# Making the low parts of layer B's weights with ScalarE and an accumulating DMA

## The chip, the cores and the metric

The kernel runs on one core of one Trainium2 chip. The metric is device time in microseconds (us) of one execution, the median of several. A core has five engines that take their instructions in order from queues of their own: TensorE (PE in the profile; its weight loads are listed as PEld), VectorE (DVE), ScalarE (ACT), GpSimd (POOL) and SyncE (SP, which here only issues DMAs). They meet through semaphores, that is, one engine's instruction waits until another engine, or a DMA, has signalled.

## The reference

The reference is a trunk of two transformer-like layers on one sequence of 512 tokens, 1024 wide, in float32, with a memory of 256 tokens. Cut to what matters:

```python
for l in range(2):
    h = rmsnorm(x, norm_mix[l])
    if l == 0:                        # layer A
        proj = h @ a_w_in[0]          # gates, values, memory queries
        main = short_conv_mixer(hv, gate_b, gate_c, a_conv[0])
    else:                             # layer B
        proj = h @ b_w_q[0]           # q1, q2 and memory queries
        q1, q2 = rope(rmsnorm(q1)), rope(rmsnorm(q2))
        o = diff_attention(q1, q2, k1, k2, v, lam)   # softmax(s1) - lam * softmax(s2)
        main = rmsnorm(o, b_subln[0]) * (1 - lam_init)
    mo = memory_attention(qm, mem_n, w_mem_kv[l], ...)
    x = x + concat(main, mo) @ w_o[l]
    x = x + square(relu(rmsnorm(x, norm_mlp[l]) @ w_up[l])) @ w_down[l]
    if l == 0:
        k1, k2, v = split(rmsnorm(x, kv_norm) @ w_kv)   # k1, k2 get rmsnorm and rope too
```

## The kernel before

Every large product is done three times over. The kernel keeps each float32 operand as two float32r tiles: the high part (the value as a float32r write leaves it) and the low part (the value minus the high part). `product` (L276) then issues three matmuls for each 128x128 weight block: high weight by high data (L279), high weight by low data (L280), low weight by high data (L281). The activations stand transposed, features on the partitions and the 512 tokens along the free dimension, so one matmul streams 512 columns.

The weights are packed on the host into `wall`, in the order of use, as a list of units (`UNITS`). A unit is eight 128x128 blocks, 512 KB. There are 192 of them: layer A (`qmA`, `mkv`, `win`, `woA`), the first MLP (`up`, `dn`), layer B (`qB`: 2 units, `qk`, `kk` and `kv`: 18 units, `wo1`: 6, `wo2`: 2) and the second MLP. The 28 units of layer B are the ones that the change touches.

`prep_to` (L251) makes a unit's weights ready one half at a time (four blocks, 128x512 elements, 256 KB):

- `dma_to` (L225) loads the raw unit through SP into one of three buffers `raw`: as one DMA (L234) or, for `qB`, `qk`, `kk` and `kv`, as two (L238). For those four kinds POOL then multiplies each half by the norm's gains (L244).
- ACT copies the half into `wh` (L261), which is the high part.
- DVE subtracts `wh` from the raw half and writes `wl`, the low part (L263). For `wo1`, and for one unit of the second MLP that is called `side`, POOL does that subtraction.

`wh` and `wl` have four buffers each, and a half is prepared three halves ahead of its use (`AHEAD`). So the writes of a half wait until PE has finished with the half four places earlier, and PE takes it up three halves after that. A raw buffer is free for the next load when both halves of its unit have been read, that is, when the second `wl` is done.

In layer B the products of the weights (`gemm_pieces`, L283; `wo1`, L972; `wo2`, L995) are interleaved with attention. A small planner (`later`, `drive`, `next_task`) runs the attention's pieces as tasks that come due after so many weight blocks. The pieces that the steps of the prediction touch are:

- head norms (`HeadNorm`, L480): ACT squares (L495, L496), DVE low parts (L497), PE sums, reciprocal roots (L416 to L420), then DVE scales the heads (L525) and `split` (L345) makes high and low parts on ACT (L346) and DVE (L347);
- rotary embedding of a pair's queries and keys: row DMAs out (L940), a DVE shuffle (L951), three POOL operations (L952 to L954), row DMAs back (L946);
- memory attention (L585): DVE maxima (L620), ACT exponentials (L623), transposes (L594), products `mov` (L603);
- differential attention (L657): score products `sc` (L583), DVE maxima (L705), ACT exponentials (L708) and scaling (L712), DVE combination `pm` (L713), PE transposes `tp` (L677), their split `th`, `tl` (L346, L347), products `o` (L690), ACT eviction (L693);
- the norm of the attention's output (`subln`, L631): ACT squares (L638, L639), DVE low part (L640), PE sums `oss` (L645, L646), root (L416 to L420), DVE scaling `ob` (L648) and split into `hh`, `hl`, which the products of `wo1` or `wo2` wait for.

What the source emits is put into each engine's queue by a scheduler when the program is built; in the trace the order on an engine is close to the order of the source, though not the same.

Of the kernel before, what the change touches and what calls it, by code (L numbers as in the profile page):

```python
# [10 lines left out]
F32 = mybir.dt.float32  # L11
F32R = mybir.dt.float32r
AF = mybir.ActivationFunctionType
ALU = mybir.AluOpType
# [21 lines left out]
WO_B = (2, 3)  # L36
SEG = 4
AHEAD = 3
LO_ON_POOL = ("wo1",)
WARM = 9  # L40

SUMS, ROOTS, NEXT_ROOT, VT = 5, 8, 3, 2
# [21 lines left out]
def _unit_list():  # L64

    u = []
    u += [("qmA", t, KT) for t in range(2)]
    for m in range(NH):
        if m == MEMA:
            u += [("mkv", 0, t, KT) for t in range(4)]  # L70
        if m == MEMB:
            u += [("mkv", 1, t, KT) for t in range(4)]
        u += [("win", CONV + m * P, KT), ("win", 2 * CONV + m * P, KT), ("win", m * P, KT)]
    u += [("woA", d, KT) for d in range(KT)]

    def mlp(l):
        r = []
        for q in range(NF):
            r += [("up", l, q * KT + f, KT) for f in range(KT)]
            r += [("dn", l, q, d, KT) for d in range(KT)]  # L80
        return r

    u += mlp(0)
    u += [("qB", 768 + t * P, KT) for t in range(2)]
    for p, t in LAYER_B:
        if t < 4:
            u += [("qk" if t < 2 else "kk", p * P + (t % 2) * 64, KT)]
        else:
            u += [("kv", 768 + (2 * p + t - 4) * P, KT)]
    u += [("wo1", i, KT) for i in range(len(WO1) // KT)]  # L90
    u += [("wo2", i, KT) for i in range(len(WO2) // KT)]
    u += mlp(1)
    return u


UNITS = _unit_list()
# [95 lines left out]
def trunk_kernel(ctx: ExitStack, tc: tile.TileContext, xT, memT, wall, cst, shp, csn, out):  # L192
    nc = tc.nc
    act, dve, pool, pe = nc.scalar, nc.vector, nc.gpsimd, nc.tensor
# [24 lines left out]
    side = next(i for i, u in enumerate(UNITS) if u[:2] == ("up", 1))  # L219
# [5 lines left out]
    def dma_to(n, between=()):  # L225
        between = list(between)
        while st["dma"] <= min(n, len(UNITS) - 1):
            i = st["dma"]
            kind, nb = UNITS[i][0], UNITS[i][-1]
            r = wpool.tile([P, KT, P], F32, tag="raw", name="raw", bufs=3)  # L230
            src = wall[OFFS[i] : OFFS[i] + P * P * nb].rearrange("(p b n) -> p b n", p=P, n=P)
            step = SEG if i < 2 or kind in ("qB", "kv", "qk", "kk") else nb
            if step == nb:
                nc.sync.dma_start(out=r[:, :nb, :], in_=src)  # L234
            for b0 in range(0, nb, step):
                rs = r[:, b0 : min(nb, b0 + step), :]
                if step < nb:
                    nc.sync.dma_start(out=rs, in_=src[:, b0 : min(nb, b0 + step), :])  # L238
                    for f in between[:2]:
                        f()  # L240
                    between = between[2:]
                if kind in ("qB", "kv", "qk", "kk"):
                    g0 = C_MIX1 if kind in ("qB", "qk") else C_KV
                    pool.tensor_tensor(  # L244
                        out=rs, in0=rs,
                        in1=cs[:, g0 + b0 : g0 + b0 + step].unsqueeze(2).to_broadcast([P, step, P]),
                        op=ALU.mult)
            st["raw"][i] = r
            st["dma"] += 1

    def prep_to(n):  # L251
        while st["prep"] <= min(n, len(halves) - 1):
            i, h = halves[st["prep"]]
            dma_to(i + 1)
            r = st["raw"][i]
            b0, b1 = h * SEG, min(UNITS[i][-1], h * SEG + SEG)
            rs = r[:, b0:b1, :]
            wh = wpool.tile([P, SEG, P], F32R, tag="wh", name="wh", bufs=4)
            wl = wpool.tile([P, SEG, P], F32R, tag="wl", name="wl", bufs=4)
            n_ = b1 - b0  # L260
            act.activation(out=wh[:, :n_, :], in_=rs, func=AF.Copy)  # L261
            eng = pool if i == side or UNITS[i][0] in LO_ON_POOL else dve
            eng.tensor_tensor(out=wl[:, :n_, :], in0=rs, in1=wh[:, :n_, :].bitcast(F32), op=ALU.subtract)  # L263
            st["w"][(i, h)] = (wh, wl)
            st["prep"] += 1

# [2 lines left out]
    def weights(b):  # L269

        i, b = cur["u"] + b // KT, b % KT
        prep_to(first[(i, b // SEG)] + AHEAD)
        wh, wl = st["w"][(i, b // SEG)]
        return wh[:, b % SEG, :], wl[:, b % SEG, :]
# [8 lines left out]
    def gemm_pieces(ps, srcs, order=range(KT), step=1, cols=slice(None)):  # L283

        u = cur["u"]
        cur["u"] += cols.stop in (None, S)
        for j, b in enumerate(order):
            prep_to(first[(u, b // SEG)] + AHEAD)
            wh, wl = (w_[:, b % SEG, :] for w_ in st["w"][(u, b // SEG)])
            product(ps, (wh, wl), [x_[:, cols] for x_ in srcs[b]], j == 0, j == len(order) - 1)  # L290
            if j % step == step - 1:
                yield
# [765 lines left out]
```

## Time and profile before

| | |
|---|---|
| median of 3 runs | 1149.05 us (1148.96 to 1150.08) |
| the profiled execution, its own time | 1151.81 us |
| its span, first to last instruction | 1150.0 us, 14438 instructions |
| PE busy over the span | 1134.6 us |
| DVE, ACT, POOL busy over the span | 660.2, 534.8, 125.4 us |
| mean granted TensorE clock | 0.995 of full speed |

The profile is one execution, recorded by the hardware. A row of the timeline gives start, duration, engine, line, operation, output and inputs; in square brackets stands how long the engine had been idle just before, and what ended that wait. A row of the groups gives how many instructions of one kind there are, their busy time together, the mean of one in ns, the idle time before them and what ended it. A row of the windows gives the busy time of PE, PEld, DVE, ACT and POOL in one stretch, then the granted TensorE clock (PEclk), the DMA engines' share and GB/s. The strips on the page cut the span into 40 equal slices of 28.75 us; each digit is the busy share in tenths. Matmuls overlap in the records: each lasts 0.39 us, while one starts every 0.23 us. So a busy PE may still lose time to small gaps, and a wait that matters shows as a bracket on a PE row.

### The profile page before, as it was taken

How to read it: one execution, taken by the hardware profiler on the slowest of the kernel's cores; microseconds unless marked ns; L12 is line 12 of the kernel's file. 1: busy time of each engine (PE TensorE's matmuls, PEld its weight loads, DVE VectorE, ACT ScalarE, POOL GpSimd, SP SyncE). 2: the span in 40 equal slices, each digit the busy share in tenths (PEclk: the TensorE clock that was granted, in tenths of full speed). 3: DMA queues.
4: the chain of work that ended last, by engine and by line, in shares of the span. 5: the costliest groups of instructions: out<-in, count | busy, mean ns of one | idle time of the engine just before them, and what ended most of it. 6: DMA issues, size and time to landing. Idle time of an engine off the chain costs nothing.

```text
span 1150.0 us, 14438 instructions
## 1 busy us (share of the span) xinstructions
PE 1134.6 (99%) x5343; PEld 929.2 (81%) x5343; DVE 660.2 (57%) x1106; ACT 534.8 (47%) x1037; POOL 125.4 (11%) x130
## 2 busy tenths in 40 slices
PE   8999999999999999999999999999999999999998
PEld 6888888888888888888887777678788888888887
DVE  7876664643453443445778899877643543443442
ACT  6656544542342342344577777666532432432431
POOL 3100002000000000003433332224000000000000
PEclk9999999999999999999999999999999999999999
DMA  7232333223322322324322123212232233223231
GB/s 267 99 111 73 103 109 101 92 92 103 99 92 95 107 92 92 106 97 137 119 83 67 62 70 106 92 56 74 94 108 92 92 101 102 92 94 106 94 112 71
DMA packets 38983, 113.64 MB, mean 99 GB/s; under 512 B 4992, under 2 KB 6528, under 8 KB 38912
## 3 DMA queue, kind: packets, MB, share of 16 engines
q1 hardware_dynamic: 38912, 112.71, 29.7%
q8 instruction: 42, 0.69, 0.2%
q14 instruction: 29, 0.24, 0.1%
HBM read 106.93 MB, written 4.19 MB: 97 GB/s over the span
## 4 chain that ended last, share of the span: by engine, by line
PE 84%; DVE 5%; ACT 2%; issue 1%; ACTq 0%; DVEq 0%
PE g L279 26%; PE g L280 26%; PE g L281 26%; PE sc L583 1%; PE mov L603 1%; PE o L690 1%; DVE wl L263 1%; DVE xl L436 1%; PE mtp L594 1%; PE msc L583 0%; DVE ra L420 0%; PE tp L677 0%; DVE dnb L705 0%; ACT pm L708 0%; DVE x L1018 0%
## 5 line engine op out<-in xcount | busy, mean ns | idle before, releaser
L261 ACT ACTIVATE wh<-raw 128x512 fp32r<-128x512 f32 x384 | 241.9, 631 | 487.5 <-PE g L280 428.8
L263 DVE TENSOR_TENSOR wl<-raw,wh 128x512 fp32r<-128x512 f32 x370 | 263.3, 712 | 175.6 <-ACT wh L261 174.6
L279 PE MATMUL g<-xh,wh 128*128 128x512 f32 x816 | 323.0, 396 | 0.4 <-DVE x L1018 0.4
L280 PE MATMUL g<-xl,wh 128*128 128x512 f32 x816 | 320.0, 392 | 3.1 <-DVE xl L436 3.0
L281 PE MATMUL g<-xh,wl 128*128 128x512 f32 x816 | 319.1, 391 | 0.0
L279 PE MATMUL g<-hh,wh 128*128 128x512 f32 (+1 forms) x632 | 246.3, 390 | 1.8 <-ACT hh L346 1.8
L280 PE MATMUL g<-hl,wh 128*128 128x512 f32 (+1 forms) x632 | 245.4, 388 | 0.0
L281 PE MATMUL g<-hh,wl 128*128 128x512 f32 (+1 forms) x632 | 245.1, 388 | 0.0
L280 PEld LDWEIGHTS g<-xl,wh 128*128 128x128 f32 x816 | 153.6, 188 | 36.8 <-DVE xl L436 6.1
L279 PEld LDWEIGHTS g<-xh,wh 128*128 128x128 f32 x816 | 153.8, 188 | 35.9 <-issue 2.5
L281 PEld LDWEIGHTS g<-xh,wl 128*128 128x128 f32 x816 | 153.6, 188 | 32.3 <-DVE wl L263 0.3
L279 PEld LDWEIGHTS g<-hh,wh 128*128 128x128 f32 x632 | 119.1, 188 | 27.4 <-ACT hh L346 2.1
L280 PEld LDWEIGHTS g<-hl,wh 128*128 128x128 f32 x632 | 119.3, 189 | 24.3 <-DVE dsm L711 0.6
L281 PEld LDWEIGHTS g<-hh,wl 128*128 128x128 f32 x632 | 119.3, 189 | 24.0
L772 DVE TENSOR_TENSOR x<-x,g 128x512 f32<-128x512 f32 (+1 forms) x65 | 44.1, 679 | 105.4 <-PE g L281 105.4
L762 DVE SCALAR_TENSOR_TENSOR v<-g,rstd 128x512 f32<-128x512 f32 x64 | 44.1, 691 | 90.7 <-PE g L281 90.7
L765 DVE TENSOR_TENSOR hl<-a,hh 128x512 fp32r<-128x512 f32 x64 | 44.4, 694 | 38.0 <-ACT a L764 38.0
L455 POOL TENSOR_TENSOR acc<-acc,sqf 128x512 f32<-128x512 f32 x18 | 24.7, 1372 | 368.6 <-ACT sqf L443 368.2
L244 POOL TENSOR_TENSOR raw<-raw,cs 128x512 f32<-128x512 f32 x40 | 45.7, 1161 | 79.8 <-DMA raw<-in_wall_dram 49.1
L763 ACT ACTIVATE hh<-v 128x512 fp32r<-128x512 f32 x64 | 40.4, 632 | 19.5 <-DVE v L762 19.5
L764 ACT ACTIVATE a<-v 128x512 f32<-128x512 f32 x64 | 39.3, 615 | 0.0
L708 ACT ACTIVATE pm<-sc,dnb 128x128 f32<-128x128 f32 (+3 forms) x48 | 24.8, 519 | 7.7 <-DVE dnb L705 7.6
(277 smaller groups left out, 1014.6 us busy)
## 6 DMA issues: line engine op xcount, KB each, us to landing
raw<-in_wall_dram SPq DMA_DIRECT2D x170, 512.0 KB, 3.5
raw<-in_wall_dram SPq DMA_DIRECT2D x44, 256.0 KB, 3.0
x<-x SPq DMA_DIRECT2D x16, 256.0 KB, 2.6
x<-in_xT_dram SPq DMA_DIRECT2D x8, 256.0 KB, 5.2
out_dram<-x SPq DMA_DIRECT2D x7, 256.0 KB, 2.1
mraw<-in_memT_dram SPq DMA_DIRECT2D x4, 256.0 KB, 5.8
rc<-qp SPq DMA_DIRECT2D x24, 32.0 KB, 1.9
qp<-rc SPq DMA_DIRECT2D x24, 32.0 KB, 2.0
```

Of the source, the lines that this page charges most:

```text
L244: pool.tensor_tensor(out=rs, in0=rs, in1=cs[:, g0 + b0 : g0 + b0 + step].unsqueeze(2).to_broadcast([P, step, P]), op=ALU.mult)
L261: act.activation(out=wh[:, :n_, :], in_=rs, func=AF.Copy)
L263: eng.tensor_tensor(out=wl[:, :n_, :], in0=rs, in1=wh[:, :n_, :].bitcast(F32), op=ALU.subtract)
L279: pe.matmul(out=ps, lhsT=wh, rhs=xh, start=start, stop=False)
L280: pe.matmul(out=ps, lhsT=wh, rhs=xl, start=False, stop=False)
L281: pe.matmul(out=ps, lhsT=wl, rhs=xh, start=False, stop=stop)
L708: act.activation(out=pm[:, m, 0:n], in_=sc[m][:, 0:n], func=AF.Exp, bias=nb[:, m : m + 1], accum_out=sm[:, m : m + 1])
L762: dve.scalar_tensor_tensor(out=v, in0=ps, scalar=0.0, in1=rstd, op0=ALU.max, op1=ALU.mult)
L763: act.activation(out=hh, in_=v, func=AF.Square)
L764: act.activation(out=a, in_=v, func=AF.Square)
L765: dve.tensor_tensor(out=hl, in0=a, in1=hh.bitcast(F32), op=ALU.subtract)
L772: dve.tensor_tensor(out=x[d][:, c], in0=x[d][:, c], in1=ps[:, c], op=ALU.add)
```

## The change

```diff
-LO_ON_POOL = ("wo1",)
+LO_BY_DMA = ("qB", "qk", "kk", "kv", "wo1", "wo2")
...
             wh = wpool.tile([P, SEG, P], F32R, tag="wh", name="wh", bufs=4)
             wl = wpool.tile([P, SEG, P], F32R, tag="wl", name="wl", bufs=4)
             n_ = b1 - b0
-            act.activation(out=wh[:, :n_, :], in_=rs, func=AF.Copy)
-            eng = pool if i == side or UNITS[i][0] in LO_ON_POOL else dve
-            eng.tensor_tensor(out=wl[:, :n_, :], in0=rs, in1=wh[:, :n_, :].bitcast(F32), op=ALU.subtract)
+            if UNITS[i][0] in LO_BY_DMA:
+
+                act.activation(out=wl[:, :n_, :], in_=rs, func=AF.Copy, scale=-1.0)
+                pool.dma_start(out=wl[:, :n_, :].bitcast(F32), in_=rs, accum_op=ALU.add)
+                act.activation(out=wh[:, :n_, :], in_=rs, func=AF.Copy)
+            else:
+                act.activation(out=wh[:, :n_, :], in_=rs, func=AF.Copy)
+                eng = pool if i == side else dve
+                eng.tensor_tensor(out=wl[:, :n_, :], in0=rs, in1=wh[:, :n_, :].bitcast(F32), op=ALU.subtract)
```

For the 56 halves of layer B's 28 units, ACT first writes minus the raw half into `wl` as float32r, which is minus the high part. A DMA that POOL issues then adds the raw half to it in place, so that `wl` holds raw minus high. ACT's copy into `wh` follows. The subtraction on DVE (44 of these halves) or POOL (the 12 halves of `wo1`) is gone. All other units keep their old way, and so does `side`.

## The prediction

> **What bounds the kernel now.** I read the page first, then busy times by stage, then PE's waits in layer B.
>
> ```profile
> span 1150.0 us, 14438 instructions
> PE 1134.6 (99%) x5343; PEld 929.2 (81%) x5343; DVE 660.2 (57%) x1106; ACT 534.8 (47%) x1037; POOL 125.4 (11%) x130
> ...
> DVE  7876664643453443445778899877643543443442
> ACT  6656544542342342344577777666532432432431
> ```
>
> PE is busy 1134.6 of 1150.0 us. An edit that leaves PE's work alone can only win what PE loses by waiting and by a slower clock. DVE is full in the slices around 630 to 720 us, which is layer B; there I asked for the stage.
>
> ```profile
> 540.00:575.00 35.00, 35.00 (x155) 28.59 (x154) 25.27 (x31) 18.17 (x32) 17.68 (x16) 1.00 0.36 121
> 575.00:775.00 200.00, 193.98 (x1022) 150.26 (x1021) 170.22 (x364) 144.65 (x351) 63.29 (x69) 0.98 0.24 77
> 775.00:815.00 40.00, 38.27 (x191) 30.71 (x191) 31.08 (x46) 23.60 (x45) 11.73 (x8) 1.00 0.24 79
> ```
>
> From 575 to 775 us, where attention runs between the products, PE misses 6.0 of 200 us and DVE is busy 85%, ACT 72%. Whom PE waits for (window 540 to 830 us):
>
> ```profile
> PE g L279 <- ACT hh L346: 1.8, 1, 1.8
> PE tp L677 <- DVE tl L347: 1.2, 1, 1.2
> PE tp L677 <- DVE pm L713: 1.2, 2, 0.6
> ...
> PE mov L603 <- ACT mp L623: 0.7, 1, 0.7
> ```
>
> Those four rows make 4.9 us, all at the end of chains that go back and forth between DVE and ACT. The weights themselves are never waited for here. So the change acts by making these chains shorter or longer, and by bringing weights late or not.
>
> **What it removes.** In the groups of 575 to 775 us:
>
> ```profile
> L261 ACT ACTIVATE wh<-raw 128x512 fp32r<-128x512 f32 x43 | 27.0, 628 | 20.3 <-PE g L280 15.5 <-issue 4.5
> L263 DVE TENSOR_TENSOR wl<-raw,wh 128x512 fp32r<-128x512 f32 x32 | 25.8, 807 | 2.6 <-ACT wh L261 2.4
> ...
> L263 POOL TENSOR_TENSOR wl<-raw,wh 128x512 fp32r<-128x512 f32 x12 | 16.0, 1336 | 42.4 <-ACT wh L261 33.8 <-PE tp L677 8.5
> ```
>
> DVE loses 32 x 0.807 = 25.8 us, and falls from 170.2 to 144.4 us of 200. POOL loses 16.0 us of subtractions. Those also slow DVE, which shows at the longest wait:
>
> ```profile
> 738.90 1.29 POOL L263 TENSOR_TENSOR wl<-raw,wh 128x512 fp32r<-128x512 f32 x1 [3.12 <-ACT wh L261]
> 740.71 1.26 POOL L263 TENSOR_TENSOR wl<-raw,wh 128x512 fp32r<-128x512 f32 x1 [0.52 <-ACT wh L261]
> ...
> 739.29 1.45 DVE L420 SCALAR_TENSOR_TENSOR ra<-ra,ry 128x512 f32<-128x512 f32 x1
> 740.77 1.75 DVE L648 SCALAR_TENSOR_TENSOR ob<-ob,sub_g,ra 128x512 f32<-128x512 f32 x1
> ...
> 743.24 0.59 PE L279 MATMUL g<-hh,wh 128*128 128x512 f32 x1 [1.75 <-ACT hh L346]
> ...
> L420 DVE SCALAR_TENSOR_TENSOR ra<-ra,ry x13: 417/674/1653, 71.2 to 784.3; 8x512 f32<-8x512 f32 x6, 128x512 f32<-128x512 f32 x5, 128x256 f32<-128x256 f32 x2
> L648 DVE SCALAR_TENSOR_TENSOR ob<-ob,sub_g,ra x7: 475/737/1749, 673.4 to 785.2; 128x512 f32<-128x512 f32 x5, 128x256 f32<-128x256 f32 x2
> ```
>
> The two DVE steps that PE waits for at 743.24 take 1.45 and 1.75 us, each beside a POOL subtraction; their medians are 0.674 and 0.737. Without the subtractions the chain is 0.78 + 1.01 = 1.79 us shorter, about the whole wait of 1.75. [...]
>
> The wait at 743.24 costs more than itself, since the clock falls behind it:
>
> ```profile
> 743.00:748.00 5.00, 4.76 (x11) 2.50 (x12) 3.76 (x11) 2.25 (x7) 0.00 (x0) 0.55 0.02 7
> 748.00:752.00 4.00, 4.00 (x19) 3.32 (x18) 1.93 (x5) 2.58 (x7) 1.53 (x3) 0.71 0.00 0
> ...
> 660.00:700.00 40.00, 37.81 (x189) 29.00 (x187) 38.55 (x77) 29.80 (x66) 13.11 (x15) 1.00 0.24 73
> ```
>
> That is 5 x 0.45 + 4 x 0.29 = 3.4 us of lost matmul time. The other waits, of which the longest is 1.23 (below), lie in stretches with a clock of 1.00; so I take 1.2 us as harmless and 1.75 as enough. [...]
>
> The three other waits have a low part's subtraction on DVE ahead of them:
>
> ```profile
> 616.76 1.40 DVE L263 TENSOR_TENSOR wl<-raw,wh 128x512 fp32r<-128x512 f32 x1
> ...
> 620.93 0.39 PE L603 MATMUL mov<-mth,mh 128*128 128x256 f32 x1 [0.65 <-ACT mp L623]
> ...
> 666.27 0.67 DVE L263 TENSOR_TENSOR wl<-raw,wh 128x512 fp32r<-128x512 f32 x1
> ...
> 668.96 0.66 PE L677 MATMUL tp<-sh,pm 128*128 128x128 f32 x4 [1.23 <-DVE tl L347]
> ...
> 690.09 0.66 DVE L263 TENSOR_TENSOR wl<-raw,wh 128x512 fp32r<-128x512 f32 x1
> ...
> 692.69 0.41 PE L677 MATMUL tp<-sh,pm 128*128 128x128 f32 x2 [0.63 <-DVE pm L713]
> ```
>
> At 620.93 the removed 1.40 covers the wait of 0.65: -0.65. At 668.96, with a wait of 1.23, the removed 0.67 shifts L713 and `tl`, but L713 also waits for ACT, so I take -0.5. At 692.69 the removed 0.66 covers 0.63: -0.6. What is late next at these places is ACT's part of the same chains.
>
> **What it adds on ACT.** One more activation per half: 43 x 0.628 = 27.0 us from 575 to 775. ACT goes from 144.7 to 171.7 of 200 us, 86%, just what DVE has now. Chains that DVE held up will now be held up by ACT, queued behind one activation more. Beside these, ACT stands still in front of a `wh` until PE frees it, and `wl` is freed one matmul later (0.23 us), so what is queued there (softmax, splits) starts up to 0.9 us later. From below this costs nothing, where ACT's idle 55 us absorb it; from above it brings back what DVE's load cost, 0.65 + 1.2 + 1.2 = 3.1 us of waits. ACT's load comes out so near to DVE's that I take a value towards the upper end, 2.5 us.
>
> **What it adds on POOL and the DMAs.** 56 DMAs of 256 KB. The trace has no DMA issued by POOL and none that adds. Issue: I take 1.3 us, POOL's subtraction (1.29), since the issue takes its place in the queue. Transfer: the nearest rows are
>
> ```profile
> raw<-in_wall_dram SPq DMA_DIRECT2D x44, 256.0 KB, 3.0
> x<-x SPq DMA_DIRECT2D x16, 256.0 KB, 2.6
> ```
>
> 2.6 us for the same size is the lower end; an adding DMA also reads what it adds to, so 2 x 2.6 = 5.2 is the upper. I take 3.0, nearer to the lower, since both rows are mostly not data: 512 KB takes little more than 256. Together 4.3 us from ACT's end, between 3.9 and 6.5. The cover is what PE still has ahead of it. The tightest place is the first half of `qB`:
>
> ```profile
> 547.36 0.39 PE L281 MATMUL g<-hh,wl 128*128 128x512 f32 x1
> ...
> 547.56 0.63 ACT L261 ACTIVATE wh<-raw 128x512 fp32r<-128x512 f32 x1 [0.62 <-PE g L280]
> ...
> 556.20 0.39 PE L281 MATMUL g<-xh,wl 128*128 128x512 f32 x1
> ```
>
> Its `wl` buffer is free at 547.75, and PE reads the new one at 556.20: 8.45 us. Less 0.25 for the start and 0.63 on ACT, 7.6 us are left for issue and transfer, and 4.3 fits, with 3.3 over for the queue on POOL. Queued behind an issue that waits for ACT are the gain multiplications (two, 2.04 us), the rotary steps and memsets; their own waits are for earlier PE work. While attention runs, PE takes longer over three halves and the cover grows. A raw buffer comes free 3.6 us later (4.3 less 0.69 on DVE). Cover:
>
> ```profile
> 547.17 0.80 SPq L238 DMA_DIRECT2D raw<-in_wall_dram  x2
> ...
> 550.01 2.04 POOL L244 TENSOR_TENSOR raw<-raw,cs 128x512 f32<-128x512 f32 x2 [1.70 <-DMA raw<-in_wall_dram]
> ...
> 558.44 0.63 ACT L261 ACTIVATE wh<-raw 128x512 fp32r<-128x512 f32 x1 [0.62 <-PE g L280]
> ```
>
> This load's gains are in at 552.05 and ACT reads it at 558.44: 6.4 us spare. So I cost the DMAs at nothing; without cover each microsecond of lateness is paid once per round of four buffers.
>
> **The sum.** -1.75 (wait at 743) - 3.4 (clock) - 0.65 - 0.5 - 0.6 = -6.9; ACT +2.5; together -4.4, with rounding -4.5. The span goes from 1150.0 to 1145.5, the profiled run from 1151.81 to 1147.3. The runs' median is 1149.05, 2.76 below the profiled run; I take the difference over: **1144.5 us**. A measurement of this kernel tells a change from none at about 0.2%, 2.3 us. The case's own range is 1140.5 (ACT's cost at nothing, -6.9, and 1.6 us more where small gaps close too) to 1146.7 (ACT's cost at 3.1 gives 1145.3; from 1146.7 on it would count as no change).
>
> **The rivals.** (1) ACT takes DVE's place altogether. For it: 86% of ACT against DVE's 85%. Against: POOL stretches DVE's rows, and ACT's stay at 0.628. The short waits stay (0), a wait of ACT as long as 1.75 keeps the clock's drop: about 1149. (2) The chain at 743 shortens, but a gap elsewhere, or the end of layer B, brings the drop: -4.5 + 3.4 = -1.1, so 1148. For it: one gap over some 1.2 us is enough, and the order of the queues may shift.
>
> (3) Slower: the weights come late. The place is where PE runs products alone, 540 to 575 and 775 to 815 us, some 12 halves, three rounds of four buffers. It decides from 7.6 us between ACT's end and the landing. At 9.6, 2 us over, PE loses 3 x 2 = 6.0, and as gaps of 2 us are over 1.75 the clock drops once, 3.4: with the forecast's -4.5 this is +4.9, **1154 us**. For it: no row shows an adding DMA, and POOL's queue has 2.04 us of multiplications and 1.29 us additions in the same stretch. Against: the upper end, 6.5, is under 7.6. An issue that had to wait out one DVE instruction, 1.75 us at most above, would come to 4.3 + 1.75 = 6.1, still under 7.6; three in a row make 9.6. [...]
>
> **How the numbers follow.** Forecast 0.52; rivals (1) and (2) 0.12 each, both within 0.2%; (3) 0.24, which is slower. Range 1140.5 to 1154.5: the forecast whole but for a tail, the same cases, and (3) up to 9.6 us; beyond that I leave about 0.13, below 0.05.
>
> **What would show it.** Right: the wait for `hh` at 743 gone or under 1.2, and PEclk 1.00 around it; DVE near 144 and ACT near 172 us in that stretch; landing within 6.5 us of ACT's end; no PE wait for a `wl`. Wrong: PE's L281 waiting for a DMA between 540 and 575, or ACT behind more than 3.1 us of PE's waits.

## The result and the profile after

| | before | after |
|---|---|---|
| median (range) | 1149.57 us (1148.96 to 1150.34, 4 runs) | 1162.13 us (1160.24 to 1164.07, 4 runs) |
| profiled execution, span | 1151.81, 1150.0 us | 1162.33, 1160.2 us |
| PE busy, mean granted clock | 1134.6 us, 0.995 | 1135.0 us, 0.993 |

The ratio is 1.0115, with a 95% interval of 1.0100 to 1.0131: the change makes the kernel about 13 us slower. The forecast was 1144.5 us in a range up to 1154.5. It was wrong, in sign as well.

What stood from L261 on stands six lines lower now. New are L263, ACT's write of minus the high part; L264, the adding DMA, and L265, ACT's `wh` beside it. The three matmuls are L285 to L287; the gains (L244) and the loads (L234, L238) keep their lines. From the page of the changed kernel come the engines' busy time, POOL's DMA queue, the group of the new DMAs and their issue row (KB each, median us from issue to landing):

```profile
PE 1135.0 (98%) x5343; PEld 931.2 (80%) x5343; DVE 630.3 (54%) x1062; ACT 560.4 (48%) x1093; POOL 154.3 (13%) x174
...
q0 software_dynamic: 8064, 14.68, 7.5%
...
L264 POOL DMA_DIRECT2D wl<-raw x56 | 51.6, 942 | 64.7 <-ACT wl L263 38.7
...
wl<-raw POOLq DMA_DIRECT2D x56, 256.0 KB, 3.5
```

PE's work is the same. The span is 10.2 us longer, of which PE's busy time makes 0.4 and its idle time 9.8 (1160.2 - 1135.0 = 25.2, where it was 1150.0 - 1134.6 = 15.4). The DMAs themselves cost no more than the prediction gave them: 0.94 us on POOL, and 3.5 from the start of the issue to the landing, where it had 4.3 for both. The same stages as before (PE, PEld, DVE, ACT, POOL busy, then PEclk):

```profile
540.00:575.00 35.00, 33.39 (x146) 26.99 (x145) 18.97 (x20) 20.52 (x36) 20.69 (x19) 1.00 0.60 149
575.00:775.00 200.00, 185.89 (x980) 145.67 (x979) 140.06 (x314) 156.79 (x377) 83.81 (x104) 0.97 0.58 133
775.00:815.00 40.00, 39.38 (x206) 31.78 (x205) 28.91 (x49) 30.31 (x62) 16.65 (x14) 1.00 0.47 117
```

From 540 to 775 us PE is busy 33.39 + 185.89 = 219.3 us, where it was 229.0. Neither DVE nor ACT is full there. The longest of PE's waits, as the view of waits sums them (us in total, times, longest):

```profile
PE g L287 <- DMA wl<-raw: 5.1, 2, 3.5
PE tp L683 <- DVE pm L719: 4.4, 1, 4.4
PE hss L516 <- DVE sl L503: 3.4, 1, 3.4
```

They make 12.9 us. The wait for `hh` at 743 is no longer among them. Behind two of these waits, the longest of each of the first two rows, the granted clock (after POOL's figures) is lower:

```profile
575.00:590.00 15.00, 11.47 (x39) 8.95 (x38) 7.06 (x9) 7.59 (x15) 8.02 (x8) 0.77 0.42 102
721.00:728.00 7.00, 6.29 (x32) 5.35 (x33) 5.29 (x15) 6.00 (x16) 3.59 (x6) 0.76 0.47 83
```

Counted as in the prediction, that is 15 x 0.23 + 7 x 0.24 = 5.1 us more. In the kernel before, the waits read there and the clock made 4.9 + 3.4 = 8.3 us. The difference, 18.0 - 8.3 = 9.7, is about the 10.2 us of the span. So two new things have to be explained: weights that come late, and steps of DVE that do.

**Late weights.** The chain of waits of the changed kernel, in order of time, runs without PE from 552 to 582 us (start, duration, what; cut to the long pieces):

```profile
552.24 3.62 DMA wl<-raw
...
556.01 3.39 DMA raw<-in_wall_dram
...
559.57 0.51 POOL raw L244
560.08 0.96 issue
561.04 3.27 DMA wl<-raw
...
564.45 3.28 DMA raw<-in_wall_dram
...
567.90 0.53 POOL raw L244
568.43 0.94 issue
569.37 3.27 DMA wl<-raw
...
572.78 4.65 DMA raw<-in_wall_dram
...
577.60 0.53 POOL raw L244
```

It goes round: an adding DMA lands and frees a raw buffer, the load into that buffer runs, POOL multiplies the gains into it, and only then is the next adding DMA issued. Each round takes 8.3 to 9.7 us (from 561.04 to 569.37, and on to 579.11), and one unit passes per round. PE uses up a unit in 24 matmuls, 5.5 us. Why the DMA waits for a load of other data, POOL's timeline shows, with a row of ACT and one of PE:

```profile
567.90 1.51 POOL L244 TENSOR_TENSOR raw<-raw,cs 128x512 f32<-128x512 f32 x1 [4.09 <-DMA raw<-in_wall_dram]
569.37 0.87 POOL L264 DMA_DIRECT2D wl<-raw  x1
569.97 1.33 POOL L244 TENSOR_TENSOR raw<-raw,cs 128x512 f32<-128x512 f32 x1
570.96 1.18 POOL L264 DMA_DIRECT2D wl<-raw  x1
577.60 1.56 POOL L244 TENSOR_TENSOR raw<-raw,cs 128x512 f32<-128x512 f32 x1 [5.46 <-DMA raw<-in_wall_dram]
579.11 0.86 POOL L264 DMA_DIRECT2D wl<-raw  x1
...
567.53 0.61 ACT L263 ACTIVATE wl<-raw 128x512 fp32r<-128x512 f32 x1
...
582.42 0.80 PE L287 MATMUL g<-xh,wl 128*128 128x512 f32 x1 [3.53 <-DMA wl<-raw]
```

POOL's queue alternates gain, DMA, gain, DMA. The DMA issued at 579.11 is the eighth; ACT had written its `wl` at 568.14. It stood 11 us behind the gain of a unit two places later, and that gain stood 5.46 us for its load. PE's wait of 3.53 us ends with this DMA. In the source the eighth DMA comes ahead of that gain; the scheduler put the gain first.

**Late steps of DVE.** SP's waits in the changed kernel, and rows of DVE's and SP's timelines:

```profile
SPq L238 <- DMA wl<-raw: 91.3, 18, 9.5
SPq L234 <- DMA wl<-raw: 65.3, 11, 10.4
```

```profile
612.34 0.01 DVE L957 LOAD_MASK_SELECT rp<-rc  x1 [7.77 <-DMA rc<-qp]
612.36 0.72 DVE L957 STREAM_SHUFFLE rp<-rc 128x512 f32<-128x512 f32 x1
612.99 0.67 DVE L503 TENSOR_TENSOR sl<-sf,sh__5140 128x512 fp32r<-128x512 f32 x1
```

```profile
608.05 0.83 SPq L238 DMA_DIRECT2D raw<-in_wall_dram  x2
608.99 1.15 SPq L946 DMA_DIRECT2D rc<-qp  x2
...
711.25 1.66 SPq L946 DMA_DIRECT2D rc<-qp  x2
```

A load that waits for its raw buffer holds up everything behind it on SP, the row DMAs of the rotary part (L946) among them. DVE had written the rows at 604.44; their DMAs were issued behind the load, at 608.99, and DVE stands 7.77 us in front of the shuffle that needs them. At 717.9 it stands 4.93 us again, but there the queue is the smaller part. The rows were written at 709.01, their DMAs issued 2.2 us later, and these landed only 6.4 and 6.0 us after their issue, where no other takes over 3.4 (all lie between 1.8 and 2.0 in the kernel before). The DMA engines are 0.88 busy from 714 to 718 us. Queued behind on DVE are `sl`, for which PE waits 3.35 us at 613.71, and `pm`, for which it waits 4.36 us at 721.71.

### The profile page after: what moved, and what is told of

Its sections match the earlier page's. It is cut to its first block, busy times and chain, and to the rows that moved or that the text cites. A ratio compares the mean times of both kernels' runs of the same rounds, so it can differ in the third digit from the quotient of the medians.

```text
span 1160.2 us, 14562 instructions
## 1 busy us (share of the span) xinstructions
PE 1135.0 (98%) x5343; PEld 931.2 (80%) x5343; DVE 630.3 (54%) x1062; ACT 560.4 (48%) x1093; POOL 154.3 (13%) x174
## 4 chain that ended last, share of the span: by engine, by line
PE 80%; DMA 4%; ACT 3%; DVE 2%; issue 1%; POOL 1%; SPq 0%; POOLq 0%; DVEq 0%; ACTq 0%
PE g L285 25%; PE g L286 25%; PE g L287 25%; DMA raw<-in_wall_dram 2%; DMA wl<-raw 2%; PE o L696 1%; PE sc L589 1%; POOL raw L244 1%; DMA rc<-qp 1%; PE mov L609 1%; DVE xl L442 1%; PE msc L589 0%; ACT pm L714 0%; PE tp L683 0%; ACT mp L633 0%
## 5 line engine op out<-in xcount | busy, mean ns | idle before, releaser
L287 PE MATMUL g<-xh,wl 128*128 128x512 f32 x816 | 320.3, 393 | 5.1 <-DMA wl<-raw 5.1
L285 PE MATMUL g<-xh,wh 128*128 128x512 f32 x816 | 324.2, 398 | 0.5 <-DVE x L1024 0.4
L269 DVE TENSOR_TENSOR wl<-raw,wh 128x512 fp32r<-128x512 f32 x326 | 227.6, 699 | 170.4 <-ACT wh L267 169.4
L285 PE MATMUL g<-hh,wh 128*128 128x512 f32 (+1 forms) x632 | 245.6, 389 | 0.0
L287 PE MATMUL g<-hh,wl 128*128 128x512 f32 (+1 forms) x632 | 244.4, 387 | 0.0
L287 PEld LDWEIGHTS g<-xh,wl 128*128 128x128 f32 x816 | 154.4, 189 | 38.5 <-DMA wl<-raw 6.0
L285 PEld LDWEIGHTS g<-xh,wh 128*128 128x128 f32 x816 | 154.6, 189 | 36.1 <-issue 2.5
L285 PEld LDWEIGHTS g<-hh,wh 128*128 128x128 f32 x632 | 118.7, 188 | 25.2 <-issue 1.2
L287 PEld LDWEIGHTS g<-hh,wl 128*128 128x128 f32 x632 | 118.7, 188 | 24.2 <-issue 0.4
L264 POOL DMA_DIRECT2D wl<-raw x56 | 51.6, 942 | 64.7 <-ACT wl L263 38.7
L244 POOL TENSOR_TENSOR raw<-raw,cs 128x512 f32<-128x512 f32 x40 | 46.1, 1171 | 71.8 <-DMA raw<-in_wall_dram 70.6
L265 ACT ACTIVATE wh<-raw 128x512 fp32r<-128x512 f32 x56 | 35.1, 628 | 17.3 <-PE g L286 16.5
```

The source lines that it names most:

```text
L244: pool.tensor_tensor(out=rs, in0=rs, in1=cs[:, g0 + b0 : g0 + b0 + step].unsqueeze(2).to_broadcast([P, step, P]), op=ALU.mult)
L264: pool.dma_start(out=wl[:, :n_, :].bitcast(F32), in_=rs, accum_op=ALU.add)
L285: pe.matmul(out=ps, lhsT=wh, rhs=xh, start=start, stop=False)
L287: pe.matmul(out=ps, lhsT=wl, rhs=xh, start=False, stop=stop)
```

## The experiments

Theory T1: the order of in-order queues. Something that waits (a gain, a load) stands ahead of what it indirectly waits for, or of what others need. Rivals: T2, ACT's 56 added activations; T3, the adding DMAs' own price, by issue or traffic. T4 came up on the way: POOL's gains behind an issue hold DVE's operations up. Unless a diff says otherwise the base is the changed kernel; ratios are to the kernel before on the same chip, with 95% intervals.

### ACT's load without the DMAs

```diff
-                pool.dma_start(out=wl[:, :n_, :].bitcast(F32), in_=rs, accum_op=ALU.add)
                 act.activation(out=wh[:, :n_, :], in_=rs, func=AF.Copy)
+                eng = pool if UNITS[i][0] == "wo1" else dve
+                eng.tensor_tensor(out=wl[:, :n_, :], in0=rs, in1=wl[:, :n_, :].bitcast(F32), op=ALU.add)
```

> ACT writes minus the high part as in the changed kernel, but DVE (GpSimd for wo1) adds the weight to it in place, and no DMA does: ACT's load of the change without its DMAs. T1: 1148-1153, near the kernel before. T2: near the changed kernel, 1159-1165. T3: near the kernel before, 1148-1153.

Measured: 1149.29 us, 0.9999 (0.9990 to 1.0008). ACT is busy 167.55 us of 575 to 775, more than in the changed kernel, and nothing is lost. T2 falls.

### One half of the change at a time

```diff
-LO_BY_DMA = ("qB", "qk", "kk", "kv", "wo1", "wo2")
+LO_BY_DMA = ("wo1", "wo2")
```

> Only the 16 halves of wo1 and wo2 (no gains on POOL) are made by ACT and an adding DMA; the 40 halves of qB, qk, kk and kv are subtracted by DVE, as before. T1: the loop needs gains and adding DMA on the same units, so it is not there, and the row DMAs stand behind loads no longer than before: 1144-1150, below or at the kernel before, as the wait at 743 goes. T2: 16 of 56 added activations, but in the stretch where ACT is fullest: 1150-1155. T3: 16 of 56 of the loss of 12.6, or 1151-1155.

Measured: 1146.54 us, 0.9972 (0.9963 to 0.9982): faster than the kernel before, by 3.2 us. Its stage with attention:

```profile
575.00:775.00 200.00, 197.14 (x1051) 153.97 (x1050) 166.84 (x368) 154.52 (x373) 59.57 (x71) 1.00 0.35 95
```

PE is busy 197.14 us, 3.2 more than before, at a clock of 1.00 in place of 0.98, and the wait for `hh` is gone. Most of this win is the clock's: over all runs its mean goes from 0.9968 to 0.9991, which is some 2.7 us of the span (an estimate from these two means). The other half:

```diff
-LO_BY_DMA = ("qB", "qk", "kk", "kv", "wo1", "wo2")
+LO_BY_DMA = ("qB", "qk", "kk", "kv")
...
-                eng = pool if i == side else dve
+                eng = pool if i == side or UNITS[i][0] == "wo1" else dve
```

> Only the 40 halves of qB, qk, kk and kv, which have gains on POOL, are made by ACT and an adding DMA; wo1 is subtracted on GpSimd and wo2 on DVE, as before. T1 and T4: these 40 hold the whole loss and give up what wo1 and wo2 alone gained (3.0 us): 1160-1166. T3 (a price for each adding DMA): 40 of 56 of the loss of 12.6, 1157-1160.

Measured: 1166.85 us, 1.0143 (1.0121 to 1.0165). PE waits 5.8 us for weights in four places and 1.8 us for `hh`. The whole loss is in the kinds that have gains on POOL, and the 16 other DMAs win; an equal price for each DMA (T3) does not fit.

### The source's order on POOL

```diff
-                    pool.tensor_tensor(
-                        out=rs, in0=rs,
+                    with tc.issue_after(st["add"]) if "add" in st else ExitStack():
+                        pool.tensor_tensor(
+                            out=rs, in0=rs,
...
-                pool.dma_start(out=wl[:, :n_, :].bitcast(F32), in_=rs, accum_op=ALU.add)
+                st["add"] = pool.dma_start(out=wl[:, :n_, :].bitcast(F32), in_=rs, accum_op=ALU.add).ins
```

> The changed kernel with one thing more: each unit's gain multiplications are queued on POOL behind the adding DMAs of the unit before, as the source writes them. T1 (POOL's queue has a unit's gains ahead of the DMA that must free the raw buffer for the next load, so that one unit of weights passes per round of some 8.4 us, where PE uses one up in 5.5): two units pass per round, the waits of 1.8 and 3.7 us at 570 to 582 go with the clock drop behind them, SP's queue stands less, and the time falls from 1162 to 1145-1153. T2 (ACT's 56 added activations make it late): no change, 1160-1164. T3 (the adding DMAs are too slow or take too much of the DMA engines): no change, 1160-1164.

Measured: 1162.62 us, 1.0123 (1.0104 to 1.0142). T1's number was missed by 10 us, yet its first half came true: no PE product waits for weights, POOL stands 12.1 us in front of gains for loads where it stood 70.6, and PE is busy 34.63 of the 35 us from 540 to 575. The longest sums of PE's waits are now for DVE's `pm` (2.8 us) and `tl` (1.9). DVE still stands once, 4.1 us, for row DMAs, and more often its own operations last long. A stretch of DVE's and of POOL's timeline in this run, 603 to 613 us:

```profile
606.27 0.67 DVE L627 TENSOR_REDUCE nb<-msc 128x2 f32<-128x512 f32 x1
606.87 3.01 DVE L427 SCALAR_TENSOR_TENSOR ra<-ra,ry 8x512 f32<-8x512 f32 x1
```

```profile
606.39 0.87 POOL L265 DMA_DIRECT2D wl<-raw  x1 [0.40 <-ACT wl L264]
607.00 2.33 POOL L245 TENSOR_TENSOR raw<-raw,cs 128x512 f32<-128x512 f32 x2
```

An operation of 0.67 us lasts 3.01, until POOL's two gains are done. Between 540 and 815 us ten operations of DVE last 2.0 to 4.5 us here; in the kernel before none lasts over 1.8, in the changed kernel three do. T4 is that DVE gets no turn where gains follow an issue directly; how much of the 13 us these operations make was not measured.

### The row DMAs away from SP

```diff
-            nc.sync.dma_start(out=c["rc"][t * 32 + m * 16 : t * 32 + m * 16 + 16, :], in_=qn[r, :])
+            act.dma_start(out=c["rc"][t * 32 + m * 16 : t * 32 + m * 16 + 16, :], in_=qn[r, :])
```

> The changed kernel, with the row DMAs of the rotary part issued from ACT's queue in place of SP's, so that they stand behind no weight load. T1: the loop of gains, adding DMA and load stays (the first waits at 570 to 582 as in the changed kernel, 5.4 us and 3.4 of clock), but DVE's stands of 7.8 and 4.9 us in front of the shuffle go, and with them PE's waits at 613 and 721 (7.8 us and 1.7 of clock): 1151-1156. T2 and T3: 1160-1164, since neither has anything to do with SP's queue.

The edit moves the rows on their way out; the DMAs that bring them back (L952) stay on SP. Measured: 1159.58 us, 1.0092 (1.0077 to 1.0107), a smaller gain than expected. The mechanism was there: DVE no longer stands in front of the shuffle, and the waits for `sl` and `pm` fall from 3.4 and 4.4 to 0.2 and 0.6 us. But PE now waits 9.1 us for weights, in five places, where it was 5.1 in two. The loop had been hidden behind the other waits. And DVE stands 8.3 us, in two places, for the rows on their way back, for which it never stood in the changed kernel. The longer stand, 5.96 us, is POOL's queue again: the shuffle was done at 666.24, but the first rotary step stood behind a gain and started at 674.29.

### Four raw buffers

```diff
-            r = wpool.tile([P, KT, P], F32, tag="raw", name="raw", bufs=3)
+            r = wpool.tile([P, KT, P], F32, tag="raw", name="raw", bufs=4)
```

and a few small tiles shared to make room.

> The changed kernel with four raw buffers in place of three (room made by sharing one scratch tile of the root, the memory's root factor and two small softmax tiles with others). T1: a load needs the landing of a DMA two units back, so the waits of PE for weights at 570 to 582 go, and SP's queue stands less: 1147-1154 if that is all. T4: the DVE operations of 2 to 3.5 us stay, so 1153-1161. T3: 1160-1164.

Measured: 1156.66 us, 1.0058 (1.0042 to 1.0075). About half of the loss goes. Two waits for weights remain (3.4 us), and DVE still stands 8.2 us for `rc` once. POOL stands in front of gains for loads nearly as long as before the edit, 68.8 us where it was 70.6: the scheduler placed the gains earlier for it. In the changed kernel POOL has mostly done the gains of three or four later halves when it issues a half's DMA; here it is five or six.

### Gain and DMA by turns

The gains of the next unit are queued one by one ahead of this unit's two DMAs: gain, DMA, gain, DMA, so that the gains of two later halves are ahead of each DMA, in place of three or four.

```diff
...
+                gains(1)
-                pool.dma_start(out=wl[:, :n_, :].bitcast(F32), in_=rs, accum_op=ALU.add)
+                queued(lambda: pool.dma_start(out=wl[:, :n_, :].bitcast(F32), in_=rs, accum_op=ALU.add))
```

> The changed kernel with POOL's queue in the order gain, adding DMA, gain, adding DMA: the loop of one unit per round is gone as with the source's order, but two gains never follow one issue. T4: DVE's long operations shrink from some 3.2 us to about 2, so part of the loss goes: 1152-1158. T1 alone: 1145-1153. T3: 1160-1164.

Measured: 1155.76 us, 1.0045 (1.0027 to 1.0063). No PE product waits for weights, as in the run before with the source's order. Of DVE's operations six last over 2 us in place of ten, five of them 2.1 to 2.6, one 5.4. DVE still stands once, 4.3 us, for row DMAs. The loss shrinks as the held operations get fewer, which agrees with T4; what else the new order changes was not separated.

### Gains on DVE

```diff
-                    pool.tensor_tensor(
+                    dve.tensor_tensor(
                         out=rs, in0=rs,
```

> The changed kernel with the 40 gain multiplications on DVE in place of POOL, which then has the adding DMAs and little else in layer B's weights. Since the run with the source's order on POOL lost as much as the changed kernel though no PE product waited for weights any more, a new theory T4 stands beside T1: a POOL multiplication directly behind the issue of an adding DMA keeps DVE's two-operand operations from finishing until POOL pauses (3.0 to 4.5 us for an operation of 0.68), and what queues behind them on DVE reaches PE late. T4: without POOL multiplications no DVE operation lasts over 2 us, the adding DMAs no longer stand behind gains, and the time is 1144-1152, though DVE carries 27 us more. T1 alone (only the order of POOL's queue): 1145-1152 too, but then the run with the source's order should have been there. T3 (the adding DMA itself, by its issue or its traffic): 1157-1164.

Measured: 1165.68 us, 1.0141 (1.0116 to 1.0165). The held operations are gone but for one over 2 us, and no product waits for weights; but the time is no better (the profiled run is the longest of the six, 1172.25). DVE's timeline (561 to 574 us) and a row of PE's:

```profile
567.45 1.29 DVE L244 TENSOR_TENSOR raw<-raw,cs 128x512 f32<-128x512 f32 x2 [5.35 <-DMA raw<-in_wall_dram]
568.66 0.74 DVE L414 SCALAR_TENSOR_TENSOR ra<-ss,eps_c,ry 128x512 f32<-128x512 f32 x1
```

```profile
572.37 0.79 PE L515 MATMUL hss<-sh__4788,indr 128*128 128x512 f32 x1 [4.25 <-ACT sh__4788 L501]
```

The same queue fault, on another engine: DVE stands 5.35 us in front of a gain for its load, the norm's root is queued behind, and PE waits 4.25 us at the end of that chain. Over the run DVE stands 35.0 us in 18 places for such loads.

### Both at once

> The changed kernel with four raw buffers and the gains on DVE, both at once. With the gains on DVE alone, DVE stood up to 5.4 us in front of a gain for its load, whose buffer an adding DMA had not yet freed: the same loop on another engine. T1 with T4 (the loop, and DVE's operations held by POOL): the fourth buffer gives each load a round more, so DVE stands little in front of gains, no operation lasts over 2.6 us, and the time is 1144-1151. T3 (the adding DMAs' own price): 1155-1164. If one of the two theories is wrong the time stays near that of four buffers alone, 1156.

The edits are those of the run with four raw buffers and of the run with the gains on DVE. Measured: 1166.75 us, 1.0148 (1.0129 to 1.0167). A miss: DVE stands 34.3 us in 17 places, as much as with three buffers. A buffer more is no cure here: with it the scheduler placed the gains earlier on DVE too.

### An issue between the gains of the kernel before

In the kernel before:

```diff
...
+                    with tc.issue_after(g) if b0 else ExitStack():
+                        if b0:
+                            g = pool.dma_start(out=scr, in_=eps_c).ins
+                    with tc.issue_after(g) if b0 else ExitStack():
+                        g = pool.tensor_tensor(
...
```

> The kernel before, with all its subtractions, and one more thing: between the two gain multiplications of a unit GpSimd issues a DMA of 8 bytes a partition into a scratch tile that nothing reads (20 of them). No buffer waits for it and it moves nothing. T4: DVE operations that start beside such an issue last 2.0 to 2.6 us, as in the alternating run, and the time rises by 1-6 us: 1150.5-1156. T1 alone, and T3 by traffic: no DVE operation over 1.9 us, and 1148.5-1150.5.

Measured: 1151.99 us, 1.0027 (1.0012 to 1.0041), at the foot of T4's range. The issue of 8 bytes a partition takes 0.58 us. Four operations of DVE last 2.1 to 2.9 us, three of them at 539 to 553 us, where PE loses little (34.78 of 35 us busy). In the kernel before none is that long. So held operations are there without any weight depending on a DMA. The edit as a whole, 20 issues and the order that it forces, costs 3.1 us by the ratio (1.4 to 4.7). The 56 of the changed kernel are longer; whether T4 alone makes the whole loss with the source's order, this run can't say.

### Late gains

```diff
-                    pool.tensor_tensor(
-                        out=rs, in0=rs,
-                        in1=cs[:, g0 + b0 : g0 + b0 + step].unsqueeze(2).to_broadcast([P, step, P]),
-                        op=ALU.mult)
+                    st["gains"][(i, b0 // SEG)] = cs[:, g0 + b0 : g0 + b0 + step].unsqueeze(2).to_broadcast([P, step, P])
...
+            if (i, h) in st["gains"]:
+                last = [x for x in nc.cur_bb.bb.instructions if x.engine == mybir.EngineType.DVE][-1]
+                with tc.issue_after(last):
+                    dve.tensor_tensor(out=rs, in0=rs, in1=st["gains"][(i, h)], op=ALU.mult)
             if UNITS[i][0] in LO_BY_DMA:
```

> The changed kernel (three raw buffers) with the gains on DVE, and each gain queued only when its half is converted, one unit later than where the load is asked for. With gains on DVE placed as early as the buffers allow, DVE stood 34 us in all in front of gains for their loads, with three raw buffers and with four. T1 in its wider form (an in-order queue holds an instruction ahead of what it indirectly waits for, whatever the engine and the number of buffers): the load has been under way for a unit when the gain's turn comes, DVE stands less than 10 us there, and the time is 1145-1153. T3 (the adding DMAs' own price): 1157-1166, since the queue would then not be the cause.

Measured: 1149.68 us, 0.9996 (0.9986 to 1.0006). The loss of 13 us is gone, with all 56 adding DMAs in place, landing in a median of 3.7 us, and with the 40 gains (a median of 0.68 us) on DVE, which is busy 643.1 us where it was 630.3. DVE stands nowhere in front of a gain for a load. The run with the gains on DVE above differs from this one only in where the gains stand in DVE's queue, and took 1165.68 us: there the place alone makes some 16 us. The stages:

```profile
540.00:575.00 35.00, 34.61 (x150) 27.68 (x150) 19.76 (x29) 18.98 (x35) 11.30 (x11) 1.00 0.61 148
575.00:775.00 200.00, 196.18 (x1034) 151.63 (x1033) 161.78 (x365) 168.95 (x403) 55.46 (x76) 1.00 0.61 139
```

T3 falls as the cause of the loss: the DMA engines are as busy as in the changed kernel (0.61), and PE works 196.18 of 200 us. For PE's weights 0.4 us of waiting is left in the whole run.

### Late gains and rows on ACT's queue

> As the run with late gains, and the rotary part's row DMAs issued from ACT's queue, so that they stand behind no weight load on SP. T1 in its wider form with the second place of it (row DMAs on SP behind loads that wait for adding DMAs): 0-4 us below the run with late gains, 1143-1152. T3: 1157-1166 as that run.

The edits are those of the run above and of the row DMAs. Measured: 1159.31 us, 1.0088 (1.0074 to 1.0102), 10 us worse than with late gains alone. A miss. 24 issues at 0.51 us now stand in ACT's queue, PE waits 4.8 us for weights in four places, and ACT itself stands 4.4 us for row DMAs. These waits are not the 10 us, though: PE's idle time is the same as with late gains alone (13.7 and 13.9 us of the span), while its busy time for the same matmuls rises from 1134.7 to 1143.8 us, at a mean clock of 0.999 in both. So the time must go in gaps between matmuls that are too small to show as waits (their records overlap), and what makes them stays open. Nothing was won by taking the rows off SP.

## Why the prediction was wrong

The step that failed is the sentence on POOL's queue: "Queued behind an issue that waits for ACT are the gain multiplications (two, 2.04 us), the rotary steps and memsets; their own waits are for earlier PE work." It looked at what stands behind the DMA, not at what stands ahead of it. For POOL's queue it had 3.3 us over; the DMA of PE's longest wait stood 11.0 us there. And the waits of the gains are for loads, not for PE: a row that the prediction itself quoted says so (L244 with "1.70 <-DMA raw<-in_wall_dram"). With the change such a load waits for an adding DMA on the same queue, and the circle is closed. "So I cost the DMAs at nothing" fell with it.

Point by point:

- Issue and transfer, forecast 4.3 us: 3.5 in the median, the issue's 0.94 among them. Right, a little high; but the longest, 7.0 us, lies above the forecast's upper end of 6.5.
- Cover of 7.6 us: right as a bound. The DMA of the longest wait landed at 582.4 (579.11 + 3.26), 14.2 us after ACT's end at 568.14; of this 3.3 are issue and transfer, and 11.0 are queue.
- Rival (3), at 0.24, had the right sign, and the wrong cause: three DVE instructions in a row against the issue, or a slow DMA. The place was right in part: PE's waits for weights end at 572.68 (1.61 us) and, past the stretch that it named, at 582.42 (3.53 us); from 775 to 815 us there is none. Its 1154 left out SP's queue and, through it, DVE. Its 9.6 is 4.3 and three DVE instructions of 1.75 us that an issue would have to wait out. No run shows such a term: the changed kernel's 56 issues last 0.85 to 1.25 us, and the 11.0 us of the longest wait's DMA are POOL's queue.
- "A raw buffer comes free 3.6 us later", covered by 6.4 us: the sum was right for one unit. It was not asked what a late load holds up behind it on SP. That gave most of the 7.77 us on DVE, and a part of the 4.93.
- The wait at 743 and the clock's drop behind it, -1.75 and -3.4: the wait is gone in the changed kernel and in the run with `wo1` and `wo2` alone, where the whole win is 3.2 us, most of it the clock's. The forecast had 4.5 for the whole change, so the size of the gain was not what failed.
- "1.75 as enough" for the clock to fall: no such bound shows. In the changed kernel the clock stays at 1.00 from 612 to 630 us, behind a wait of 3.35 us at 613.71, and falls behind those of 3.53 and 4.36.
- DVE near 144 and ACT near 172 us: 140.06 and 156.79. The stage holds 41 of ACT's `wl` there, since the work came later; in the two runs where PE was not held up it holds 45, and ACT is busy 167.55 and 168.95.
- ACT's +2.5: the run with ACT's load and no DMA gives 0.9999, so ACT's price and DVE's gain about cancel; neither was measured alone.

What stays open: what share of the 13 us is POOL's queue, SP's queue, the slow landing at 717 and T4 each, since mending one uncovered the next. On DVE the place of the gains is shown to make the loss; on POOL the source's order freed the weights and not the time, and what late gains on POOL would give was not tried.

## What to carry to other kernels

When an operation goes from an engine to a DMA on an in-order queue, draw the circle: which buffer does its landing free, which load waits for that buffer, what waits for that load, and does any of it stand ahead of the same DMA on the same queue? Read it from the queue's order as built, not from the source: here the scheduler had built another. A buffer more helped by half with the gains on POOL and not at all with them on DVE; in both, the gains were placed earlier for it. On DVE, placing them later took the loss away.

## What was not expected of the hardware

With the source's order a two-input DVE operation lasted through several POOL instructions in a row: 3.01 us for 0.67, beside one issue and two gains. The gains ended at 609.33 (607.00 + 2.33), the operation 0.55 us later. Two more of that run, of 3.37 and 3.22 us, end 0.56 and 0.57 us after the two gains beside them. None of the three ended between its two gains. In the kernel before, POOL's gains stand in pairs too (2.04 us), and no operation of DVE there lasts over 1.8 us; what the issue ahead of them changes was not settled.
